# Head-pair values shifted and centred with tokens on partitions instead of by centring products

## The chip, the cores and the metric

The kernel runs on one core of one Trainium2 chip. The metric is the device time of one execution in microseconds (us); the time before is the median of three runs. Engine names follow the profile: PE is TensorE (PEld its weight loads), DVE is VectorE, ACT is ScalarE, POOL is GpSimd, SP is the engine whose queue issues nearly all DMAs.

## The reference, cut to what matters

One layer: a combined projection of a 256-token stream (4096 wide), sixteen heads of forgetting attention, thirty-two heads of an RWKV-7 recurrence of width 64, a SiLU gate, an output projection and a LayerNorm. The change touches the recurrence's values `vr`: the projected values are first mixed with those of the token before, and the recurrence's output is normalised over the 64 channels of each head.

```python
proj = einsum('bsd,dc->bsc', x, w_in)
rw_prev = pad(rw, one zero token in front)[:, :-1]
rw = rw + (rw_prev - rw) * mu_shift
S_t = S_{t-1} diag(decay_t) + (S_{t-1} a_t) b_t^T + v_t k_t^T ;  y_t = S_t r_t
mu = mean(y over the head's 64 channels)
y = (y - mu) * rsqrt(var + GN_EPS) * gn_gain + gn_bias
```

The output is linear in the values, so taking the mean over a head's 64 channels out of the values takes it out of `y` as well. The kernel does that: the recurrence runs on centred values, and no mean has to be taken of `y`. The bonus term uses the values uncentred.

## The kernel before, in words

The input projection is eight passes (n = 0 to 7) of four blocks (b = 0 to 3), each block 512 output columns. A block contracts 4096 in 16 steps of two 128-row tiles. Its weights come in 512 KB pieces, named `w<n>_<b>_<q>` and shown by the profile as `w_<q>`: SP fetches a piece into one of four raw buffers (`fetch`, L212), ACT rounds it to a high part (`split`, L139, four buffers, `w_<q>h`), DVE forms the rest (L140, three buffers, `w_<q>l`), and PE makes twelve products of a step out of them: x high by w high (L145), x low by w high (L146), x high by w low (L147), for two token halves and two tiles. With these buffers DVE can form the low part of a piece only when PE has left the piece three before it.

Block 0 of a pass gives r and k of two head groups, block 1 the recurrent values (columns 0 to 255) and the attention's values (256 to 511) with tokens on partitions, blocks 2 and 3 the rest. At a block's end ACT copies the sums to `bk` (L784 for block 1), and `unload` (L697) turns them to channels on partitions by PE transposes (`tr`, L711) and mixes in the token before (`lerp`, L256: ACT L257, DVE L258, tile `s`). This and everything else, the recurrence (`rwkv`, L464), its preparation (`prepare`) and the attention (`fox`), is written as generators that take a turn at each `slot` inside a block. A scheduler then sets the final order of each engine's instructions from that; each engine and the SP queue works strictly in its own order.

Where the change sits, in block 2 of each pass: `rwkv` makes 32 products `gp` (L476), then 32 products `vp` (L485) that turn the shifted values `s` back to tokens on partitions and centre them at once, their moving operand the constant `cent` (identity minus 1/64 inside a head). DVE masks `gp` into `gb` (L496) and `lt` (L504), ACT copies `vp` to `SV` and `UV` (L510, L511), DVE multiplies `bon` by `s` (L513), POOL scales `BK` (L479), PE transposes `BK` (`tp`, L521). SP carries `gb` to DRAM and back (`nd`, `Nb`, L499 and L500).

Of the kernel before, what the change touches and what calls it, by code (L numbers as in the profile page):

```python
# [10 lines left out]
F32 = mybir.dt.float32  # L11
# [3 lines left out]
ALU = mybir.AluOpType  # L15
AX = mybir.AxisListType

P = 128
S = 256
D = 4096  # L20
KT = D // P
G = 16
C = 64
NCH = S // C
HD = 64
# [25 lines left out]
C_ID = 0  # L51
C_MASK = 128
C_ONES = 256
C_CENT = 384
C_E = 512
C_SCAN = 640
C_ROW = C_SCAN + S
C_W = C_ROW + 2
# [3 lines left out]
def constants():  # L62
    p = np.arange(P)[:, None]
    s = p % C
    t = np.arange(C)[None, :]
    cst = np.zeros((P, C_W), np.float32)
    cst[:, C_ID : C_ID + P] = np.eye(P)
    cst[:, C_MASK : C_MASK + C] = s < t
    cst[:, C_MASK + C : C_MASK + 2 * C] = s <= t
    same = (np.arange(P)[:, None] // HD) == (np.arange(P)[None, :] // HD)  # L70
    cst[:, C_ONES : C_ONES + P] = same
    cst[:, C_CENT : C_CENT + P] = np.eye(P) - same / HD
    j = (p % NG) * NJ + np.arange(P)[None, :] // B
    cst[:, C_E : C_E + P] = j == np.arange(P)[None, :] % B
    cst[:, C_SCAN : C_SCAN + S] = (np.arange(S)[None, :] % C) != 0
    first = np.array([1, 1, 0, 1, 0], np.float32)
    cst[:5, C_ROW] = 2 * first - 1
    cst[:5, C_ROW + 1] = 1 - first
    return cst


@with_exitstack
def layer(ctx: ExitStack, tc: tile.TileContext, xt, xtok, w_lora, w_main, w_o, up, par, mulora, fbias, lng, lnb, cst, out):
    nc = tc.nc
    PS = bass.MemoryType.PSUM

# [6 lines left out]
    def pst(name):  # L93
        return ps.tile([P, 512], F32, tag="ps", name=name)

    cs = const.tile([P, C_W], F32, name="cs")
# [31 lines left out]

    ident = cs[:, C_ID : C_ID + P]
    ones = cs[:, C_ONES : C_ONES + P]  # L130
    cent = cs[:, C_CENT : C_CENT + P]

    def column(name, i):
        return prm[:, PAR.index(name), i : i + 1]
# [21 lines left out]
    for n, (k0, k1) in enumerate(pieces):  # L156
        for k in range(k0, k1):
            t = xpool.tile([P, 2, S], F32R, tag=f"x{k}", name=f"x{k}")
# [31 lines left out]
    def wait(n):  # L190
        for _ in range(n):
            yield
# [50 lines left out]
    rp = mid.enter_context(tc.tile_pool(name="rp", bufs=1))  # L243
# [116 lines left out]
    HALF = [slice(0, C), slice(C, P)]  # L360
# [5 lines left out]
        return t.rearrange("p a b -> p (a b)")  # L366

    rk = {}
    pairs = {}
    done = set()  # L370
    prepared = set()
# [92 lines left out]
    def rwkv(n):  # L464
# [7 lines left out]
        for u in range(2):  # L472
            for c in range(NCH):
                for j in range(2):
                    h = HALF[j]
                    nc.tensor.matmul(gp[u][j][:, c * P : (c + 1) * P], BK[h, u, c, :], lt[j][h, u, c, :], start=True, stop=True)  # L476
        v = vv[n]
        kept = BK[:, :, 0 : NCH - 1, :]
        nc.gpsimd.tensor_tensor(kept, kept, lc[:, :, 0 : NCH - 1].unsqueeze(3).to_broadcast([P, 2, NCH - 1, P]), ALU.mult)  # L479
        vp = pst(f"vp{n}")  # L480
        for u in range(2):
            for c in range(NCH):
                for j in range(2):
                    h, o = HALF[j], HALF[1 - j]
                    nc.tensor.matmul(vp[o, u * S + c * C : u * S + (c + 1) * C], v[:, u, c * C : (c + 1) * C], cent[:, h], start=True, stop=True)  # L485

        def m(rows):
            return cs[rows, C_MASK : C_MASK + P].unsqueeze(1).to_broadcast([C, NCH, P])

# [3 lines left out]
        for u in range(2):  # L493
            for j in range(2):
                h = HALF[j]
                nc.vector.tensor_tensor(gb[j][h, u], gv[u][j][h], m(h), ALU.mult)  # L496
            for a in range(4):
                o = B * (a % 2)
                nc.sync.dma_start(out=nd[u, a].rearrange("c r s -> r c s"), in_=gb[a // 2][B * a : B * (a + 1), u, :, o : o + B])  # L499
            nc.sync.dma_start(out=flat(nb[:, u]), in_=nd[u].rearrange("q c r s -> (q c) (r s)").unsqueeze(1).to_broadcast([16, NG, B * B]))  # L500
        for u in range(2):
            for j in range(2):
                o = HALF[1 - j]
                nc.vector.tensor_tensor(lt[j][o, u], gv[u][j][o], m(o), ALU.mult)  # L504
        SV = [rp.tile([P, 2, NCH, C], F32, tag=f"SV{j}", name=f"SV{j}_{n}") for j in range(2)]
        UV = [rp.tile([P, 2, NCH, C], F32, tag=f"UV{j}", name=f"UV{j}_{n}") for j in range(2)]
        for j in range(2):
            o = HALF[1 - j]
            vo = vp.rearrange("p (u c t) -> p u c t", u=2, t=C)[o]
            nc.scalar.copy(SV[j][o], vo)  # L510
            nc.scalar.copy(UV[j][o], vo)  # L511
            nc.gpsimd.memset(SV[j][HALF[j], :, 0, :], 0.0)
        nc.vector.tensor_tensor(flat(bon), flat(bon), flat(v), ALU.mult)  # L513
        for u in range(2):
# [9 lines left out]
        prod = rp.tile([P, 2, NJ, B], F32, tag="prod", name=f"prod{n}")  # L524
# [20 lines left out]
        for a in range(4):  # L545
            o = C * (a // 2) + B * (a % 2)
# [3 lines left out]
        for u in range(2):  # L550
            for c in range(NCH):
                for j in range(2):
                    a, b = slice(C * j, C * j + B), slice(C * j + B, C * j + C)
                    nc.tensor.matmul(qp[b, u * P + c * B : u * P + (c + 1) * B], gb[j][a, u, c, B:C], T[a, u, c, :], start=True, stop=True)
        Q = rp.tile([P, 2, NCH, B], F32, tag="xc", name=f"Q{n}")
        for j in range(2):
            b = slice(C * j + B, C * j + C)
# [27 lines left out]
        for c in range(NCH):  # L585
# [10 lines left out]
            if c < NCH - 1:  # L596
# [4 lines left out]
                for j in range(2):  # L601
                    h = HALF[j]
# [26 lines left out]
        vs = pst(f"vs{n}")  # L629
# [64 lines left out]

    unloading = []

    def unload(n, b, bk, vt):  # L697
        yield from wait(LAG)
        if b == 0:
            while n and 2 * n - 1 not in prepared:  # L700
                yield
        elif b == 2:
            while n and n - 1 not in done:
                yield
        fq = fk = None
        cols = BLOCKS[b]
        for h in range(len(cols) // 2):
            tr = pst(f"tr{n}_{b}_{h}")
            for t in range(2):
# [48 lines left out]
    res = None  # L758
# [16 lines left out]
    vt = None  # L775
    for n in range(G // 2):
        for b in range(4):
            acc = block(n, b)
            while unloading:
                slot()  # L780
            bk = rp.tile([P, 2, OB], F32, tag="bk", name=f"bk{n}_{b}")
            for m in range(2):
                if b == 1:
                    nc.scalar.copy(bk[:, m, : 2 * P], acc[m][:, : 2 * P])  # L784
                else:
                    nc.scalar.copy(bk[:, m, :], acc[m])
            if b == 1:
                while n and 2 * n - 1 not in foxed:
                    slot()
                vt = rp.tile([P, 2, 2 * P], F32, tag="vt", name=f"vt{n}")  # L790
                for m in range(2):
                    nc.scalar.copy(vt[:, m, :], acc[m][:, 2 * P :])
            unloading.append(n)
            side(unload(n, b, bk, vt))
# [104 lines left out]
def arrange(inputs):  # L899
    a = {n: np.asarray(v) for n, v in inputs.items()}  # L900
# [11 lines left out]
    tiles = np.stack([t.reshape(KT, P, G // 2, 2, P) for t in types])  # L912
    main = np.stack([np.stack([tiles[j, :, :, :, u] for j, u in c], 3) for c in cols])
    res["w_main"] = np.ascontiguousarray(main.transpose(3, 0, 2, 1, 4, 5)).reshape(G // 2, 4, P, KT, OB)
    wo = a["w_out"].reshape(2, G, P, NB, OB)
    res["w_o"] = np.ascontiguousarray(wo.transpose(3, 2, 1, 0, 4).reshape(NB, P, KT, OB))
    res["up"] = np.ascontiguousarray(np.stack([a["w_up"].reshape(LORA, G, P).transpose(1, 0, 2), a["a_up"].reshape(LORA, G, P).transpose(1, 0, 2)], 2))
# [26 lines left out]
```

## Time and profile before

| What | Value |
|---|---|
| Median of three runs | 1979.7 us (1979.61 to 1979.78) |
| Profiled execution | 1979.63 us |
| Its span in the trace | 1977.8 us, so 1.8 us lie around it |
| PE busy | 1966.3 us, 99% of the span |
| DVE, ACT, POOL busy | 1323.6, 1002.4, 34.3 us |
| DMA queue q1 | 64.3% of 16 engines' span |

Each number is of one profiled execution. A row of the timeline gives a start, a duration, the engine, the line of the kernel, what is written and read, and in brackets the engine's idle time just before it with what ended it. Products are pipelined on PE: a row's duration is longer than the distance to the next row's start, and the distance is what a product costs.

### The profile page before, as it was taken

The numbers are of one execution on the slowest core, as the hardware profiler recorded it, in microseconds if no ns is written. First come the engines' busy times: TensorE is split into PE (matmuls) and PEld (weight loads), VectorE is DVE, ScalarE is ACT, GpSimd is POOL, SyncE is SP. The second block draws the span as 40 slices with busy tenths as digits, with TensorE's granted clock in tenths as the row PEclk, the third lists the DMA queues.
The fourth block names the chain that finished last, engine by engine and source line by source line (L and its number), as shares of the span: only waits on it lengthen the run. The fifth ranks groups of instructions, "written<-read, shape, count | busy, mean of one in ns | idle before, by whom it ended". The sixth has DMA issues, their size and how long they took to land.

```text
span 1977.8 us, 28676 instructions
## 1 busy us (share of the span) xinstructions
PE 1966.3 (99%) x10624; PEld 1614.2 (82%) x10624; DVE 1323.6 (67%) x2091; ACT 1002.4 (51%) x1506; POOL 34.3 (2%) x82
## 2 busy tenths in 40 slices
PE   9999999999999999999999999999999999999998
PEld 7888788878887888788878887888788878888885
DVE  6678576857685768576857685768576856755555
ACT  6554564456445644564456445644564454433331
POOL 0100000000000000000000000000000000000000
PEclk9999999999999999999999999999999999999998
DMA  9566566656665666566656765676556777866664
GB/s 335 150 190 184 179 191 195 181 177 191 204 187 162 192 192 195 166 191 195 188 170 191 206 185 162 191 206 186 163 189 189 242 274 246 267 193 192 182 207 152
DMA packets 140429, 387.63 MB, mean 196 GB/s; under 512 B 32200, under 2 KB 42456, under 8 KB 140288
## 3 DMA queue, kind: packets, MB, share of 16 engines
q1 hardware_dynamic: 139856, 385.37, 64.3%
q8 instruction: 83, 1.36, 0.3%
q10 hardware_dynamic: 432, 0.43, 0.1%
q14 instruction: 58, 0.48, 0.1%
HBM read 371.82 MB, written 13.91 MB: 195 GB/s over the span
## 4 chain that ended last, share of the span: by engine, by line
PE 99%; DVE 1%; ACT 0%; DMA 0%; ACTq 0%; issue 0%; DVEq 0%; SPq 0%
PE acc L145 24%; PE acc L147 24%; PE acc L146 23%; PE oacc L754 6%; PE oacc L755 6%; PE oacc L756 6%; PE tr L711 1%; PE yp L616 1%; PE gp L476 1%; PE up L591 1%; PE rh L564 1%; PE sp L600 0%; PE vp L485 0%; DVE res L871 0%; PE accl L147 0%; PE tp L521 0%
## 5 line engine op out<-in xcount | busy, mean ns | idle before, releaser
L535 DVE TENSOR_REDUCE xc<-prod 128x8 f32<-128x16 f32 (+30 forms) x248 | 73.1, 295 | 6.1
L532 DVE TENSOR_TENSOR prod<-Nb,xc 128x8 f32<-128x8 f32 (+30 forms) x248 | 72.3, 292 | 7.1
L140 DVE TENSOR_TENSOR w_9l<-w,w_9h 128x1024 fp32r<-128x1024 f32 x31 | 38.1, 1228 | 46.1 <-ACT pT L670 29.0
L140 DVE TENSOR_TENSOR w_1l<-w,w_1h 128x1024 fp32r<-128x1024 f32 x31 | 37.9, 1224 | 35.4 <-PE acc L147 35.4
L140 DVE TENSOR_TENSOR w_0l<-w,w_0h 128x1024 fp32r<-128x1024 f32 x31 | 37.9, 1223 | 34.1 <-PE acc L147 25.4
L139 ACT CAST w_1h<-w 128x1024 fp32r<-128x1024 f32 x31 | 32.7, 1056 | 55.1 <-PE acc L146 38.7
L140 DVE TENSOR_TENSOR w_11l<-w,w_11h 128x1024 fp32r<-128x1024 f32 x31 | 38.0, 1225 | 33.6 <-PE acc L147 24.7
L140 DVE TENSOR_TENSOR w_3l<-w,w_3h 128x1024 fp32r<-128x1024 f32 x31 | 37.8, 1220 | 31.8 <-PE acc L147 31.8
L139 ACT CAST w_2h<-w 128x1024 fp32r<-128x1024 f32 x31 | 32.7, 1056 | 49.3 <-PE acc L146 45.5
L139 ACT CAST w_11h<-w 128x1024 fp32r<-128x1024 f32 x31 | 32.6, 1051 | 49.6 <-DMA w<-in_w_main_dram 22.9
L140 DVE TENSOR_TENSOR w_6l<-w,w_6h 128x1024 fp32r<-128x1024 f32 x31 | 37.8, 1221 | 28.5 <-ACT UV L594 13.9
L139 ACT CAST w_0h<-w 128x1024 fp32r<-128x1024 f32 x31 | 32.7, 1056 | 44.8 <-PE acc L146 38.7
L140 DVE TENSOR_TENSOR w_10l<-w,w_10h 128x1024 fp32r<-128x1024 f32 x31 | 37.9, 1224 | 26.0 <-PE acc L147 25.8
L139 ACT CAST w_13h<-w 128x1024 fp32r<-128x1024 f32 x31 | 32.7, 1054 | 43.0 <-PE acc L146 26.6
L140 DVE TENSOR_TENSOR w_2l<-w,w_2h 128x1024 fp32r<-128x1024 f32 x31 | 37.9, 1222 | 22.6 <-PE acc L147 22.4
L145 PE MATMUL acc<-w_4h,x 128*128 128x512 f32 x124 | 53.0, 428 | 0.0
L140 DVE TENSOR_TENSOR w_15l<-w,w_15h 128x1024 fp32r<-128x1024 f32 x31 | 37.8, 1220 | 22.3 <-PE acc L147 20.8
L140 DVE TENSOR_TENSOR w_12l<-w,w_12h 128x1024 fp32r<-128x1024 f32 x31 | 37.5, 1209 | 21.4 <-PE acc L147 21.4
L139 ACT CAST w_15h<-w 128x1024 fp32r<-128x1024 f32 x31 | 32.6, 1051 | 36.9 <-PE acc L146 35.3
L145 PE MATMUL acc<-w_1h,x 128*128 128x512 f32 x124 | 51.2, 413 | 0.0
L145 PE MATMUL acc<-w_6h,x 128*128 128x512 f32 x124 | 51.2, 413 | 0.0
L145 PE MATMUL acc<-w_2h,x 128*128 128x512 f32 x124 | 51.0, 411 | 0.0
(804 smaller groups left out, 6536.9 us busy)
## 6 DMA issues: line engine op xcount, KB each, us to landing
w<-in_w_main_dram SPq DMA_DIRECT2D x496, 512.0 KB
wo<-in_w_o_dram SPq DMA_DIRECT2D x128, 512.0 KB
Nb<-nd SPq DMA_DIRECT2D x16, 512.0 KB
wr<-in_w_main_dram SPq DMA_DIRECT2D x15, 512.0 KB
hd<-hl SPq DMA_DIRECT2D x29, 256.0 KB
h<-hd SPq DMA_DIRECT2D x29, 256.0 KB
res<-in_xtok_dram SPq DMA_DIRECT2D x16, 256.0 KB
xr<-in_xt_dram SPq DMA_DIRECT2D x15, 256.0 KB
```

The source lines that it names most:

```text
L139: nc.scalar.copy(hi[:, :n], src[:, :n])
L140: nc.vector.tensor_tensor(lo[:, :n], src[:, :n], hi[:, :n].bitcast(F32), ALU.subtract)
L145: nc.tensor.matmul(acc[:, :n], xs[k][:, 0, tt], hi[:, o : o + n], start=(k == 0), stop=False)
L146: nc.tensor.matmul(acc[:, :n], xs[k][:, 1, tt], hi[:, o : o + n], start=False, stop=False)
L147: nc.tensor.matmul(acc[:, :n], xs[k][:, 0, tt], lo[:, o : o + n], start=False, stop=(k == KT - 1))
L476: nc.tensor.matmul(gp[u][j][:, c * P : (c + 1) * P], BK[h, u, c, :], lt[j][h, u, c, :], start=True, stop=True)
L532: first = nc.vector.tensor_tensor(prod[:, :, :, s + 1 :], nb[:, :, s : s + 1, s + 1 :].to_broadcast([P, 2, NJ, w]), xc[:, :, :, s + 1 :], ...
L535: nc.vector.tensor_reduce(xc[:, :, :, s : s + 1], prod[:, :, :, s:], AX.X, ALU.add)
L564: nc.tensor.matmul(rh[HALF[j], u * C : (u + 1) * C], lt[j][:, u, c, 0:C], SV[j][:, u, c, :], start=True, stop=True)
L754: nc.tensor.matmul(acc, ht[k][:, 0, tt], hi[:, o], start=(k == 0), stop=False)
L755: nc.tensor.matmul(acc, ht[k][:, 1, tt], hi[:, o], start=False, stop=False)
L756: nc.tensor.matmul(acc, ht[k][:, 0, tt], lo[:, o], start=False, stop=(k == KT - 1))
```

## The change: what it does

The 32 products `vp` of each pass go, and with them the constant `cent` and the two ACT copies from `vp` to `SV`. In their place stands work on `bk` of block 1, with tokens on partitions:

- At the end of block 0, SP loads the mixing coefficients of the pass's 256 value columns into `muv` (128 KB, one DRAM row to all partitions). It takes the buffer that `prod` and `T` use later in the pass.
- At the end of block 1, POOL zeroes the first row of a new tile `vs`, and SP copies `bk` into `vs` one partition further: 127 partitions by 2 by 256 numbers (254 rows of 1 KB) in one transfer, and the one row that crosses from token 127 to token 128 in a second one.
- Two slots later POOL forms `vs = (vs - bk) * muv + bk` in three passes of 128x512.
- DVE sums `vs` over each head's 64 channels (`vm`, 128x8), and eight DVE instructions of 64x2x64 write `vs` minus a 64th of that into `SV`. ACT copies `SV` to `UV`.

The values with channels on partitions (`tr` and `lerp`) stay, since the bonus uses them.

```diff
-        vp = pst(f"vp{n}")
-        for u in range(2):
-            for c in range(NCH):
-                for j in range(2):
-                    h, o = HALF[j], HALF[1 - j]
-                    nc.tensor.matmul(vp[o, u * S + c * C : u * S + (c + 1) * C], v[:, u, c * C : (c + 1) * C], cent[:, h], start=True, stop=True)
...
+        vm = rp.tile([P, 2, 2, 2], F32, tag="vm", name=f"vm{n}")
+        vt = vs_[n].rearrange("p m (u j v) -> p m u j v", u=2, j=2)
+        nc.vector.tensor_reduce(vm.rearrange("p m u j -> p (m u j)"), vs_[n].rearrange("p m (a v) -> p (m a) v", v=HD), AX.X, ALU.add)
         for j in range(2):
             o = HALF[1 - j]
-            vo = vp.rearrange("p (u c t) -> p u c t", u=2, t=C)[o]
-            nc.scalar.copy(SV[j][o], vo)
-            nc.scalar.copy(UV[j][o], vo)
+            for c in range(2):
+                h = HALF[c]
+                for a in range(2):
+                    nc.vector.scalar_tensor_tensor(
+                        SV[j][o, :, 2 * a + c, :], vm[h, a, :, j].unsqueeze(2).to_broadcast([C, 2, HD]), -1.0 / HD, vt[h, a, :, j, :], ALU.mult, ALU.add
+                    )
+            nc.scalar.copy(UV[j][o], SV[j][o])
...
+    def token_values(n, bk):
+        p = bk[:, :, : 2 * P]
+        t = vs_[n]
+        nc.gpsimd.tensor_tensor(t, t, p, ALU.subtract)
+        nc.gpsimd.tensor_tensor(t, t, muvs[n].unsqueeze(1).to_broadcast([P, 2, 2 * P]), ALU.mult)
+        nc.gpsimd.tensor_tensor(t, t, p, ALU.add)
...
     def unload(n, b, bk, vt):
         yield from wait(LAG)
+        if b == 1:
+            token_values(n, bk)
...
+            if b == 0:
+                muvs[n] = rp.tile([P, 2 * P], F32, tag="prod", name=f"muv{n}")
+                nc.sync.dma_start(out=muvs[n], in_=muv[n : n + 1, :].to_broadcast([P, 2 * P]))
             if b == 1:
+                vs_[n] = rp.tile([P, 2, 2 * P], F32, tag="vs", name=f"vs{n}")
+                nc.gpsimd.memset(vs_[n][0:1, 0, :], 0.0)
+                nc.sync.dma_start(out=vs_[n][1:P], in_=bk[0 : P - 1, :, : 2 * P])
+                nc.sync.dma_start(out=vs_[n][0:1, 1, :], in_=bk[P - 1 : P, 0, : 2 * P])
```

The order on three engines, in pass n = 1. On PE, at the gp products of block 2, before:

```order
L476 MATMUL gp_1_1_3233<-lt_1_2786,BK_2784 128x128
L485 MATMUL vp_3251<-cs,s_2_3171 64x64 x16
L145 MATMUL acc_2_0_3134<-w_2_4h,x_364 128x512
L146 MATMUL acc_2_0_3134<-w_2_4h,x_364 128x512
L147 MATMUL acc_2_0_3134<-w_2_4l,x_364 128x512
```

The same place on PE with the change:

```order
L474 MATMUL gp_1_0_3241<-lt_1_2787,BK_2786 128x128
L474 MATMUL gp_1_1_3242<-lt_1_2788,BK_2786 128x128
L142 MATMUL acc_2_0_3140<-w_2_4h,x_364 128x512
L143 MATMUL acc_2_0_3140<-w_2_4h,x_364 128x512
L144 MATMUL acc_2_0_3140<-w_2_4l,x_364 128x512
```

The products `vp` are gone (a row counts pairs); nothing else on PE has moved, here or elsewhere. Next DVE, at the start of block 2, before (`w_2_4l` is the low part of block 2's piece 4, `s_2` the values with channels on partitions):

```order
L140 TENSOR_TENSOR w_2_3l<-w_2_3_3154,w_2_3h 128x1024
L258 SCALAR_TENSOR_TENSOR s_2_3171<-tr_1_0_3166,prm,s_2_3171 128x255
L140 TENSOR_TENSOR w_2_4l<-w_2_4_3182,w_2_4h 128x1024
L258 SCALAR_TENSOR_TENSOR s_2_3171<-tr_1_0_3166,prm,s_2_3171 128x255
L513 TENSOR_TENSOR bon_2787<-bon_2787,s_2_3171 128x512
L140 TENSOR_TENSOR w_2_5l<-w_2_5_3200,w_2_5h 128x1024
L140 TENSOR_TENSOR w_2_6l<-w_2_6_3218,w_2_6h 128x1024
L496 TENSOR_TENSOR gb_838<-gp_0_0_3230,cs 64x512
```

The same place on DVE with the change:

```order
L137 TENSOR_TENSOR w_2_3l<-w_2_3_3160,w_2_3h 128x1024
L255 SCALAR_TENSOR_TENSOR s_2_3180<-tr_1_0_3175,prm,s_2_3180 128x255
L500 TENSOR_REDUCE vm_3284<-vs_3133 128x8
L255 SCALAR_TENSOR_TENSOR s_2_3180<-tr_1_0_3175,prm,s_2_3180 128x255
L137 TENSOR_TENSOR w_2_4l<-w_2_4_3191,w_2_4h 128x1024
L506 SCALAR_TENSOR_TENSOR SV_1_3280<-vm_3284,vs_3133 64x2x64 x4
L506 SCALAR_TENSOR_TENSOR SV_1_3281<-vm_3284,vs_3133 64x2x64
L137 TENSOR_TENSOR w_2_5l<-w_2_5_3209,w_2_5h 128x1024
L506 SCALAR_TENSOR_TENSOR SV_1_3281<-vm_3284,vs_3133 64x2x64 x3
L511 TENSOR_TENSOR bon_2789<-bon_2789,s_2_3180 128x512
L137 TENSOR_TENSOR w_2_6l<-w_2_6_3227,w_2_6h 128x1024
L487 TENSOR_TENSOR gb_838<-gp_0_0_3239,cs 64x512
```

The sum over `vs` now stands ahead of the low parts of pieces 4, 5 and 6, and the eight `SV` writes between them. Last the SP queue at the end of block 1, before:

```order
L216 DMA w_2_3_3154<-in_w_main_dram 128x1024
L216 DMA w_2_4_3182<-in_w_main_dram 128x1024
L216 DMA w_2_5_3200<-in_w_main_dram 128x1024
L216 DMA w_2_6_3218<-in_w_main_dram 128x1024
L216 DMA w_2_7_3307<-in_w_main_dram 128x1024
```

The same place on the SP queue with the change:

```order
L213 DMA w_2_4_3191<-in_w_main_dram 128x1024
L213 DMA w_2_5_3209<-in_w_main_dram 128x1024
L803 DMA vs_3133<-bk_1_3130 1x16x16
L802 DMA vs_3133<-bk_1_3130 127x2x256
L213 DMA w_2_6_3227<-in_w_main_dram 128x1024
L213 DMA w_2_7_3307<-in_w_main_dram 128x1024
```

The two transfers into `vs` stand between the fetches of pieces 5 and 6 of block 2. The row of one partition is written as sixteen parts of sixteen numbers; the 127 partitions stand as they are.

More of the change, by code (lines that the diff above doesn't have):

```diff
@@ L53 @@
 C_ONES = 256
-C_CENT = 384
-C_E = 512
+C_E = 384
 C_SCAN = 640
@@ L71, in constants @@
     cst[:, C_ONES : C_ONES + P] = same
-    cst[:, C_CENT : C_CENT + P] = np.eye(P) - same / HD
     j = (p % NG) * NJ + np.arange(P)[None, :] // B
@@ L82, in layer @@
 @with_exitstack
-def layer(ctx: ExitStack, tc: tile.TileContext, xt, xtok, w_lora, w_main, w_o, up, par, mulora, fbias, lng, lnb, cst, out):
+def layer(ctx: ExitStack, tc: tile.TileContext, xt, xtok, w_lora, w_main, muv, w_o, up, par, mulora, fbias, lng, lnb, cst, out):
     nc = tc.nc
@@ L130, in layer @@
     ones = cs[:, C_ONES : C_ONES + P]
-    cent = cs[:, C_CENT : C_CENT + P]
     def column(name, i):
@@ L368, in layer @@
     rk = {}
+    vs_ = {}
     pairs = {}
@@ L695, in layer @@
     unloading = []
+    muvs = {}
+    def token_values(n, bk):
[4 more added lines that the diff above has]
+        nc.gpsimd.tensor_tensor(t, t, p, ALU.add)
     def unload(n, b, bk, vt):
         yield from wait(LAG)
+        if b == 1:
+            token_values(n, bk)
         if b == 0:
@@ L914, in arrange @@
     res["w_main"] = np.ascontiguousarray(main.transpose(3, 0, 2, 1, 4, 5)).reshape(G // 2, 4, P, KT, OB)
+    res["muv"] = np.ascontiguousarray(a["mu_shift"][4096:6144].reshape(G // 2, 2 * P))
     wo = a["w_out"].reshape(2, G, P, NB, OB)
```

## The prediction

> **What bounds the kernel now.** I read the page first: the busy times and the chain that ended last.
>
> ```profile
> PE 1966.3 (99%) x10624; PEld 1614.2 (82%) x10624; DVE 1323.6 (67%) x2091; ACT 1002.4 (51%) x1506; POOL 34.3 (2%) x82
> PE 99%; DVE 1%; ACT 0%; DMA 0%; ACTq 0%; issue 0%; DVEq 0%; SPq 0%
> ```
>
> PE bounds it: it never runs dry between the first weights and the tail, and every other engine works under its cover. So a product taken off PE is worth its pitch on PE, and any other work costs nothing as long as PE's next weights are ready. Two questions follow: what the vp products cost on PE, and how much cover DVE, ACT, POOL and SP have where the new work goes. I read both in pass 1, start of block 2, which repeats in every pass; the timeline of PE there:
>
> ```profile
> 317.53 0.39 PE L147 MATMUL acc<-w_15l,x 128*128 128x512 f32 x1
> 329.35 0.39 PE L146 MATMUL acc<-w_4h,x 128*128 128x512 f32 x1
> 329.58 0.39 PE L147 MATMUL acc<-w_4l,x 128*128 128x512 f32 x1
> 330.57 2.06 PE L476 MATMUL gp<-lt,BK 64*128 64x128 f32 x32
> 332.56 1.15 PE L485 MATMUL vp<-cs,s 128*64 128x64 f32 x32
> 333.64 0.50 PE L145 MATMUL acc<-w_4h,x 128*128 128x512 f32 x1
> 337.88 0.39 PE L145 MATMUL acc<-w_6h,x 128*128 128x512 f32 x1
> 341.51 0.39 PE L145 MATMUL acc<-w_7h,x 128*128 128x512 f32 x1
> ```
>
> Block 1's last product starts at 317.53; at 329.58 PE first needs the low part of piece 4, and at 341.51 it begins piece 7. The 32 vp products cost 333.64 - 332.56 = 1.08 us. The timelines of DVE and of ACT in the same stretch:
>
> ```profile
> 318.01 1.23 DVE L140 TENSOR_TENSOR w_2l<-w,w_2h 128x1024 fp32r<-128x1024 f32 x1 [1.49 <-PE acc L147]
> 322.98 0.48 DVE L258 SCALAR_TENSOR_TENSOR s<-tr,prm,s 128x255 f32<-128x255 f32 x1 [1.02 <-ACT s L257]
> 323.86 1.23 DVE L140 TENSOR_TENSOR w_4l<-w,w_4h 128x1024 fp32r<-128x1024 f32 x1 [0.40 <-PE acc L147]
> 325.52 0.69 DVE L513 TENSOR_TENSOR bon<-bon,s 128x512 f32<-128x512 f32 x1
> 331.77 1.41 DVE L496 TENSOR_TENSOR gb<-gp,cs 64x512 f32<-64x512 f32 x2 [1.16 <-PE gp L476]
> 337.29 1.21 DVE L140 TENSOR_TENSOR w_7l<-w,w_7h 128x1024 fp32r<-128x1024 f32 x1
> ```
>
> ```profile
> 318.68 0.37 ACT L784 COPY bk<-acc 128x256 f32<-128x256 f32 x1
> ...
> 333.76 0.58 ACT L510 COPY SV<-vp 64x512 f32<-64x512 f32 x1 [3.56 <-PE vp L485]
> ```
>
> The low part of piece 4 is done at 325.09, and PE needs it at 329.58: 4.5 us of cover. That of piece 7 is done at 338.50, needed at 341.51 + 0.46 = 341.97: 3.5 us.
>
> **What goes.** Eight times 1.08 us of PE, 8.6 us on the path. ACT loses two copies of 0.58 us per pass and its 3.56 us wait for vp; it is not on the path, so nothing.
>
> **What comes, work alone.** POOL's nearest row, and DVE's (the sums and a write into SV):
>
> ```profile
> L479 POOL TENSOR_TENSOR BK<-BK,lc 128x768 f32<-128x768 f32 x8 | 11.8, 1472 | 303.8 <-DVE gb L496 303.8
> L661 DVE TENSOR_REDUCE fst<-lg 128x1 f32<-128x256 f32 x16 | 6.5, 409 | 0.0
> L661 DVE TENSOR_REDUCE fst<-lg 128x1 f32<-128x128 f32 x16 | 4.4, 276 | 0.0
> L607 DVE TENSOR_TENSOR SV<-sp,sl 64x128 f32<-64x128 f32 x32 | 9.2, 287 | 8.3 <-PE sp L600 8.1
> ```
>
> A POOL pass over 128x512 is 1.472 x 512/768 = 0.98 us, three are 2.9 (at most 4.4, the unscaled row). The sum over 512 numbers is 0.409 + 2 x 0.133 = 0.68 us; eight SV writes at 0.287 are 2.3 us. With `vs` there in time, all of it fits in DVE's idle time: no cost. Of SP's three new transfers `muv` has a whole block until its use; its 128 packets, at the dearest price below (179 ns), keep the 16 engines for 1.4 us, with several pieces under way: nothing. The two into `vs` wait on SP for ACT's copy, with the fetch of piece 6 queued behind; but that one had to wait for the low part of piece 2 in any case, done at 318.01 + 1.23 = 319.24. The two issues before it, 0.8 us, are hidden by the time until PE uses piece 6 at 337.88.
>
> **The transfer into vs, the deciding term.** It can't start before ACT's second copy of `bk` is done at 318.68 + 0.37 = 319.05. DVE's sum waits for POOL, POOL for this transfer; and behind the sum, in DVE's strict order, stands the low part of piece 4, which PE needs at 329.58. So the 4.5 us of cover are no longer cover for short work but the budget of a chain: two issues, a landing, POOL, the sum.
>
> How long does it take to land 254 rows of 1 KB? First the rows of the DMA view, in three short windows (299.5 to 300: pieces alone; 304 to 304.5: nearly only the 1 KB rows of `upt`; 203 to 204: mostly one DRAM row sent to all partitions), then an issue on SP and SP's wait for a transfer to land:
>
> ```profile
> DMA packets 50, 0.20 MB, mean 410 GB/s; under 512 B 0, under 2 KB 0, under 8 KB 50
> q1 hardware_dynamic: 50, 0.20, 99.4%
> ...
> DMA packets 25, 0.02 MB, mean 45 GB/s; under 512 B 6, under 2 KB 24, under 8 KB 25
> q1 hardware_dynamic: 25, 0.02, 13.0%
> ...
> DMA packets 106, 0.17 MB, mean 166 GB/s; under 512 B 13, under 2 KB 79, under 8 KB 106
> q1 hardware_dynamic: 106, 0.17, 118.8%
> ...
> 300.35 0.42 SPq L378 DMA_DIRECT2D upt<-in_up_dram  x1
> SPq L543 <- DMA td<-xc: 15.0, 8, 3.2
> ```
>
> A packet occupies one engine of the 16 for share x 16 x window / packets: 0.994 x 8000/50 = 159 ns for 4 KB, so 40 ns per KB; 0.13 x 8000/25 = 42 ns for the 1 KB rows; 1.188 x 16000/106 = 179 ns where one DRAM row is read over and over. Ours reads SBUF row by row, so I take 42 ns. Over 16 engines that is 254/16 x 42 ns = 0.7 us; on one engine 254 x 42 ns = 10.6 us. No transfer of before has a row count like 127, so the trace doesn't show which. I take one engine: 127 is prime and can't be cut into equal parts, and the order hands it over whole, while it cuts the one-row transfer beside it into sixteen parts. Every large transfer of before has 128, 96 or 32 rows.
>
> The Trainium skill speaks against this change at just this place: "DMA: Bandwidth & Descriptors", section "Why a DMA increments its semaphore by 16 and not by 1", says that such a DMA runs on the largest number of engines up to 16 that divides its slowest dimension, with 127 partitions on one as an example. At the page's roughly 27 GiB/s an engine I estimate 9.0 us instead of 10.6, and the sum below would be about 2035. No run here shows it yet.
>
> So vs lands at 319.05 + 2 x 0.42 (issues) + 1.9 (15.0/8, the mean wait for a landing) + 10.6 = 332.4. POOL is done at 335.4 (ACT's copies to `prod`, which now wait for `muv` to be free, and the second `s` and the high parts of pieces 5 and 6 behind them, are released a POOL pass earlier and ready in time), DVE's sum at 336.1, the second `s` at 336.6 (0.48), the low part of piece 4 at 337.8 (1.23). PE, stopped since 329.58, has lost 8.2 us.
>
> Then PE goes from 337.8 to piece 7 in 0.99 (to gp), 1.99 (gp) and 341.51 - 333.64 = 7.87: it is there at 348.65 and needs the low part at 349.1. DVE gets there at 337.8 + 2.3 (SV) + 0.69 (bon) + 2.46 (pieces 5 and 6) + 5.52 (masks, 331.77 to 337.29) + 1.21 = 350.0, a second stop of 0.9, with which piece 7 would begin at 349.5, 8.0 us later than before. POOL's next work, BK's scaling for `tp`, waits for gp (340.8) and for the SV writes (341.3) and is done by 342.8; `tp` stands behind piece 5 and half of piece 6 on PE: no cost.
>
> PE's clock covers that second stop and adds a little. The windows of the tail, the third number from the end of a row (PEclk) being the clock, and the warm-up:
>
> ```profile
> core 0: us, PE busy (x) PEld busy (x) DVE busy (x) ACT busy (x) POOL busy (x), PEclk, DMA share, GB/s
> 1962.00:1964.00 2.00, 1.60 (x6) 0.69 (x5) 1.79 (x4) 0.00 (x0) 0.00 (x0) 1.00 0.40 162
> 1964.00:1966.00 2.00, 0.28 (x1) 0.09 (x1) 1.47 (x7) 0.29 (x1) 0.00 (x0) 0.64 0.25 100
> 1966.00:1968.00 2.00, 1.66 (x5) 1.26 (x5) 2.00 (x4) 0.26 (x1) 0.00 (x0) 0.50 0.14 55
> 1.31 2.74 PE L106 MATMUL warmup<-idle 128*128 128x512 bf16 x6 [1.31 <-POOL idle L103]
> ```
>
> With about 2 us of idle time the clock falls to 0.50, and at the start six products of 512 columns took 2.74 us, 0.457 each, against the 0.23 from 329.35 to 329.58. So an 8 us stop is followed by at least 2.7 us at half speed, a loss of 1.4 us. Then PE begins piece 7 at 350.05, needs the low part at 350.5 and finds it ready at 350.0. Shift of a pass: 350.05 - 341.51 = 8.5 us, vp's saving included. Nothing later in the pass wins it back, as PE is the bound; DVE, ACT and SP shift along. Pass 0 has the same order with two BK writes more behind the sum, within half a microsecond of this.
>
> **Sum.** 1979.6 (the profiled execution, 1979.63; the median is 1979.7) + 8 x 8.5 = 1979.6 + 68 = 2048. Bounds of this case: 40 ns a packet and no landing time, no clock loss but the second stop, gives 8.0 - 1.9 - 0.4 = 5.7 a pass, 2025; a landing of 3.2 us (the longest) and twice the clock loss gives 8.5 + 1.3 + 1.4 = 11.2, 2069. At 179 ns a packet it would be 35 us more a pass, about 2330; I keep that as a far end only.
>
> **Rivals.**
>
> Spread transfer, faster: the 254 rows go over 16 engines. Then vs lands at 319.05 + 0.84 + 1.9 + 0.7 = 322.5, POOL is done at 325.5, piece 4's low part at 327.9, before 329.58; piece 7's at 327.9 + 12.2 = 340.1, needed at 340.9 with vp gone. PE never stops, and the whole saving shows: 1979.6 - 8.6 = 1971. It decides by a landing before about 323.3, 4.2 us after the copy. For it: a 256 KB transfer of 128 rows would do this. Against it: 127. Chance 0.13.
>
> Two engines: 254 rows as two lots of 127. The transfer takes 5.3 us, PE stops about 3 us at piece 4 and 0.9 at piece 7, and I take no loss of clock: 8.0 - 5.3 = 2.7 a pass, 2001. Nothing in the order cuts the transfer so. Chance 0.05.
>
> The stop isn't PE's: the transfer takes 10.6 us, but DVE's order is of no matter, as PE would stop only for piece 6, fetched behind `vs` on the same queue. Piece 6 would land 8 x 159 ns behind vs, at 333.7, its two parts be ready 2 x 1.23 later at 336.2 and be needed at 337.88 - 1.08 = 336.8: no stop, 1971 again. It fails if the sum really stands ahead of piece 4, as the order has it. Chance 0.02, counted with the first.
>
> **How the numbers follow.** One engine 0.80 (2025 to 2069 by its own bounds, and some tens more if packets are slower), spread or hidden 0.15, two engines 0.05. To leave out no more than 2 in 10, the range takes in the two-engine case below and a margin above for slow packets: 1996 to 2095. A measurement of this kernel can tell about 0.2% (4 us) from no change. Faster by more takes the spread case with hardly a stop, 0.12; a spread case that gives its 8.6 us back in small stops, 0.03 within 0.2%; slower 0.85.
>
> **What would show it.** Right: one wait of about 8 us on PE before a product of w_4l in every pass, the row of DVE's sum (the line of `vm`) waiting for POOL, POOL's first pass waiting for `vs` about 13 us after ACT's copy, PEclk below 1 behind each stop, and the mean DMA share near 1/16 for 10 us in which only `vs` moves. Wrong: POOL starting within 4 us of the copy, and PE at 99% as before.

## The result and the profile after

| | before | after |
|---|---|---|
| median, 4 runs each (us) | 1979.65 (1978.91 to 1979.78) | 2082.16 (2079.56 to 2083.15) |
| ratio, 95% interval | | 1.0516 (1.0502 to 1.0529) |
| profiled execution: time, span (us) | 1979.63, 1977.8 | 2079.56, 2077.7 |
| mean granted PE clock | 0.997 | 0.974 |

The change costs 102.5 us, 5.2%. The forecast was 2048, its range 1996 to 2095. The page of the changed kernel, the busy times and the chain that ended last by engine and by line:

```profile
PE 1976.6 (95%) x10368; PEld 1618.9 (78%) x10368; DVE 1341.4 (65%) x2163; ACT 994.6 (48%) x1490; POOL 67.6 (3%) x114
PE 89%; DMA 6%; POOL 1%; DVE 1%; issue 1%; ACT 0%; DVEq 0%; POOLq 0%; SPq 0%
```

PE makes 256 products fewer and is busy longer, because part of its work ran at half clock. It is no longer the whole chain: a DMA holds 6% of it, about 125 us, where before its share was 0%. The waits view says for whom:

```profile
POOL vs L700 <- DMA vs<-bk: 319.1, 8, 54.0
DVE vm L500 <- POOL vs L702: 120.4, 8, 15.2
ACT prod L526 <- POOL vs L701: 114.6, 8, 15.1
PE acc L144 <- DVE w_4l L137: 88.8, 8, 11.5
```

Rows 1, 2 and 4 are the chain of the forecast, eight times each: POOL waits for the transfer into `vs`, DVE's sum (`vm`) for POOL, and PE for the low part of piece 4, which stands behind the sum on DVE. The first row's long total is harmless (POOL has nothing else to do); the last row is the cost. Row 3 is a second branch: ACT's copy to `prod` waits for POOL too, and ACT's second part of `s` stands behind it. Pass 1 in the timelines of ACT, POOL, DVE and PE, one stretch of each (start, duration, then what ran, in brackets the idle time before it and what ended that):

```profile
331.52 0.37 ACT L793 COPY bk<-acc 128x256 f32<-128x256 f32 x1
...
347.31 1.26 POOL L700 TENSOR_TENSOR vs<-vs,bk 128x512 f32<-128x512 f32 x1 [39.50 <-DMA vs<-bk]
...
349.99 1.26 POOL L702 TENSOR_TENSOR vs<-vs,bk 128x512 f32<-128x512 f32 x1
...
351.29 0.69 DVE L500 TENSOR_REDUCE vm<-vs 128x8 f32<-128x512 f32 x1 [14.98 <-POOL vs L702]
351.89 0.47 DVE L255 SCALAR_TENSOR_TENSOR s<-tr,prm,s 128x255 f32<-128x255 f32 x1
352.28 1.22 DVE L137 TENSOR_TENSOR w_4l<-w,w_4h 128x1024 fp32r<-128x1024 f32 x1
...
353.55 0.80 PE L144 MATMUL acc<-w_4l,x 128*128 128x512 f32 x1 [10.97 <-DVE w_4l L137]
```

ACT's copy is done at 331.89; the values land 15.4 us later; POOL and DVE need 6.2 us more; PE stands still for 10.97 us. What moved the values is read in the DMA view, here 335 to 340:

```profile
DMA packets 103, 0.12 MB, mean 24 GB/s; under 512 B 0, under 2 KB 102, under 8 KB 102
q1 hardware_dynamic: 102, 0.10, 6.5%
```

A share of 6.5% of 16 engines is one engine (1/16 is 6.25%), with 102 packets of 1 KB in 5 us, one each 49 ns. So the transfer of 127 rows does run on one engine, and the rule of the Trainium skill that the prediction named ("DMA: Bandwidth & Descriptors", section "Why a DMA increments its semaphore by 16 and not by 1") agrees with the trace. The page's rate (section "Specifications"), roughly 27 GiB/s an engine, gives an estimate of 9.0 us for 254 rows; the 49 ns measured here give 12.4. Last the windows view, whose third number from the end is the granted clock:

```profile
353.50:356.00 2.50, 2.45 (x8) 1.61 (x10) 2.43 (x7) 0.61 (x1) 0.00 (x0) 0.50 0.51 129
357.00:358.00 1.00, 1.00 (x22) 1.00 (x20) 1.00 (x2) 0.89 (x3) 0.10 (x1) 1.00 0.78 135
```

Behind the stop PE runs at half clock, and is at full clock again some 3.5 us after it started.

Where all of it went is best seen by the step of PE from the first product of one weight piece to the first of the next. Against before, one step of each pass grew, piece 4 of block 2, in passes 0 to 7 by 13.29, 11.67, 12.73, 11.65, 12.65, 13.22, 11.98 and 12.83 us. That is 100.0 together, against 99.9 between the two profiled executions: nothing is left to find elsewhere.

### The profile page after: what moved, and what is told of

The parts are those of the page before. It is cut to its first block, busy times and chain, and to the rows that moved or that the text cites. A ratio compares the mean times of both kernels' runs of the same rounds, so it can differ in the third digit from the quotient of the medians.

```text
span 2077.7 us, 28297 instructions
## 1 busy us (share of the span) xinstructions
PE 1976.6 (95%) x10368; PEld 1618.9 (78%) x10368; DVE 1341.4 (65%) x2163; ACT 994.6 (48%) x1490; POOL 67.6 (3%) x114
## 4 chain that ended last, share of the span: by engine, by line
PE 89%; DMA 6%; POOL 1%; DVE 1%; issue 1%; ACT 0%; DVEq 0%; POOLq 0%; SPq 0%
PE acc L142 22%; PE acc L144 21%; PE acc L143 21%; DMA vs<-bk 6%; PE oacc L763 6%; PE oacc L765 6%; PE oacc L764 6%; PE gp L474 1%; PE tr L720 1%; PE yp L614 1%; PE up L589 1%; PE rh L562 1%; POOL vs L702 0%; POOL vs L700 0%; POOL vs L701 0%
## 5 line engine op out<-in xcount | busy, mean ns | idle before, releaser
L144 PE MATMUL acc<-w_4l,x 128*128 128x512 f32 x124 | 53.8, 434 | 88.8 <-DVE w_4l L137 88.8
L144 PEld LDWEIGHTS acc<-w_4l,x 128*128 128x128 f32 x124 | 25.3, 204 | 97.6 <-DVE w_4l L137 92.1
L500 DVE TENSOR_REDUCE vm<-vs 128x8 f32<-128x512 f32 x8 | 5.5, 686 | 120.4 <-POOL vs L702 120.4
```

The lines of the kernel that those rows point to most:

```text
L144: nc.tensor.matmul(acc[:, :n], xs[k][:, 0, tt], lo[:, o : o + n], start=False, stop=(k == KT - 1))
```

## The experiments

Theory: the transfer is slow because it runs on one engine, and it costs because DVE's sum, behind it, is queued ahead of the low part of piece 4. Rivals: the time goes into holding back the weight fetches behind the transfer in SP's queue, whatever DVE does; or into POOL's and DVE's added work itself. The kernel before ran beside each group, at 1979.5 to 1979.7; all ratios are to it.

**1. The transfer cut in two, 112 and 15 rows.** The large part can now be spread.

```diff
-                nc.sync.dma_start(out=vs_[n][1:P], in_=bk[0 : P - 1, :, : 2 * P])
+                nc.sync.dma_start(out=vs_[n][1:113], in_=bk[0:112, :, : 2 * P])
+                nc.sync.dma_start(out=vs_[n][113:P], in_=bk[112 : P - 1, :, : 2 * P])
```

> The 127-row transfer cut into 112 and 15 rows, the rest of the change kept. Theory (the one-engine transfer holds DVE's sum and so PE): 112 rows go over 16 engines, 15 over 15, vs lands within 4 us of ACT's copy instead of 15.4, PE doesn't stop at piece 4, and the whole saving of the vp products shows: 1971, ratio to before 0.996. Rival (POOL's three passes of 1.26 us and the new DVE work hold PE by themselves): PE still stops in block 2, and the time is 1985 or more.

Measured: 1973.9 us, ratio 0.9971 (0.9959 to 0.9982). The timelines of ACT, POOL and DVE in pass 1:

```profile
320.11 0.36 ACT L793 COPY bk<-acc 128x256 f32<-128x256 f32 x1
...
323.75 1.30 POOL L700 TENSOR_TENSOR vs<-vs,bk 128x512 f32<-128x512 f32 x1 [27.36 <-DMA vs<-bk]
325.13 1.29 POOL L701 TENSOR_TENSOR vs<-vs,muv 128x512 f32<-128x512 f32 x1
326.50 2.15 POOL L702 TENSOR_TENSOR vs<-vs,bk 128x512 f32<-128x512 f32 x1
...
325.29 2.21 DVE L137 TENSOR_TENSOR w_4l<-w,w_4h 128x1024 fp32r<-128x1024 f32 x1 [0.40 <-PE acc L144]
```

The values land 3.3 us after the copy, 12 us sooner, and 108 us of 2082 are gone. Two things changed, though: the scheduler now also put the sum, which ran at 328.68, behind the low part of piece 4. Run 5 changes the order without the cut, run 8 uses one order with both cuts; no run has the cut with the order of the changed kernel.

**2. The cut at 96 and 31 rows.** The same edit with 97 for 113 and 96 for 112; the smaller part, 31 rows, again on one engine.

> The same transfer cut into 96 and 31 rows; 31 is prime like 127. Theory (a row count without a divisor goes to one engine): 62 packets of 47 ns on one engine, 2.9 us, on top of the 3.4 us that a landing takes besides its packets; POOL starts 6 to 7 us after the copy, some 3 us later than with 112 and 15. The chain then ends at about piece 4's or 7's need: 1971 to 1980. Rival (the row count is of no matter, only the number of rows): POOL starts as early as with 112 and 15.

Measured: 1999.2 us, ratio 1.0099 (1.0084 to 1.0114). The values landed 7.5 us after the copy (expected 6 to 7) against 3.3 in run 1, so the row count matters; the time was far off. The longest of PE's waits, and the timelines of ACT and DVE in pass 1:

```profile
PE acc L144 <- DVE w_7l L137: 14.7, 8, 2.1
```

```profile
332.51 0.30 ACT L526 COPY prod<-cs 128x128 f32<-128x128 f32 x1 [6.31 <-POOL vs L701]
332.72 0.47 ACT L254 ACTIVATE s<-tr,omm 128x256 f32<-128x256 f32 x1
...
333.22 0.48 DVE L255 SCALAR_TENSOR_TENSOR s<-tr,prm,s 128x255 f32<-128x255 f32 x1 [4.88 <-ACT s L254]
333.88 0.69 DVE L500 TENSOR_REDUCE vm<-vs 128x8 f32<-128x512 f32 x1 [0.18 <-POOL vs L702]
...
345.03 1.21 DVE L137 TENSOR_TENSOR w_7l<-w,w_7h 128x1024 fp32r<-128x1024 f32 x1
```

A second queue is at work, which the expectation had left out: ACT's copy to `prod` waits for POOL (`muv` lies in the same buffer), ACT's part of `s` stands behind it, DVE's part of `s` waits for that, and pieces 5, 6 and 7 are queued behind. Read alone, this doesn't say whether the orders or the transfer made the stops; run 8 does.

**3. The products alone taken out.** The kernel before without `vp`; its output is not the reference's, since the values it copies to `SV` and `UV` are neither turned nor centred.

```diff
-                    nc.tensor.matmul(vp[o, u * S + c * C : u * S + (c + 1) * C], v[:, u, c * C : (c + 1) * C], cent[:, h], start=True, stop=True)
...
-            vo = vp.rearrange("p (u c t) -> p u c t", u=2, t=C)[o]
+            vo = v.rearrange("p u (c t) -> p u c t", t=C)[o]
```

> The kernel before without the vp products: ACT copies the shifted values with channels on partitions into SV and UV, so the values are neither turned nor centred; nothing else is changed. The term of the sum alone: 8 x 1.08 = 8.6 us less on PE, 1971.0. Rival (a product taken off PE is filled by waiting for weights): 1979.7, no change.

Measured: 1970.6 us, ratio 0.9955 (0.9938 to 0.9971). The products are worth 9.0 us. This kernel is the floor for the rest: what a variant of the change takes above 1970.6 is the price of getting the values by another way.

**4. The transfer alone.** The kernel before, plus the two transfers into `vs`, with no reader.

```diff
+                vsn = rp.tile([P, 2, 2 * P], F32, tag="vs", name=f"vs{n}")
+                nc.gpsimd.memset(vsn[0:1, 0, :], 0.0)
+                nc.sync.dma_start(out=vsn[1:P], in_=bk[0 : P - 1, :, : 2 * P])
+                nc.sync.dma_start(out=vsn[0:1, 1, :], in_=bk[P - 1 : P, 0, : 2 * P])
```

> The kernel before with the two transfers into vs at the end of block 1 and nothing that reads vs. In the profile of the changed kernel the fetch of piece 6, issued right behind, began to move only about 8 us later, when half of the packets of vs were gone, and landed behind them. If that hold costs by itself: piece 6 lands 16 us after the copy, its low part keeps DVE from the masks, piece 7's low part is about 2.5 us late, 8 x 2.5 = 20 us: 2000. Rival (the transfer costs only through the sum that waits for it): 1979.7.

Measured: 2012.6 us, ratio 1.0169 (1.0154 to 1.0184). A transfer that nobody waits for costs 33 us. PE's longest wait, then the timelines of ACT and DVE in pass 1: the copy of `bk`, the conversion of piece 6 and its low part:

```profile
PE tp L521 <- DVE lt L504: 18.8, 16, 1.5
```

```profile
322.71 0.37 ACT L784 COPY bk<-acc 128x256 f32<-128x256 f32 x1
...
340.44 1.05 ACT L139 CAST w_6h<-w 128x1024 fp32r<-128x1024 f32 x1 [9.65 <-DMA w<-in_w_main_dram]
...
341.52 1.23 DVE L140 TENSOR_TENSOR w_6l<-w,w_6h 128x1024 fp32r<-128x1024 f32 x1 [9.61 <-ACT w_6h L139]
```

Piece 6, queued on SP behind the transfer, lands 17.4 us after the copy. DVE's masks `gb` and `lt` are queued behind its low part, and PE waits for them before `tp`; the expectation had the masks right but put the stop at piece 7 and the time at 2000. So the rival of the held fetch is real; in the changed kernel it doesn't show, because PE already stands at piece 4 while piece 6 is late.

**5. The order alone.** The changed kernel with its one-engine transfer; the sum, the `SV` writes and the `UV` copies moved behind the wait for the decay products, kept there, and ACT's copies to `prod` and `xc` kept in place.

```diff
-        nc.vector.tensor_reduce(vm.rearrange("p m u j -> p (m u j)"), vs_[n].rearrange("p m (a v) -> p (m a) v", v=HD), AX.X, ALU.add)
...
         yield from wait(W["d1"])
+        tc.keep_in_program_order(nc.vector.tensor_reduce(vm.rearrange("p m u j -> p (m u j)"), vs_[n].rearrange("p m (a v) -> p (m a) v", v=HD), AX.X, ALU.add))
...
-            nc.scalar.copy(prod[:, u], ev)
+            tc.keep_in_program_order(nc.scalar.copy(prod[:, u], ev))
```

> The changed kernel with its transfer as it is (127 rows, all on one DMA engine), but VectorE's sum over the shifted values, its eight centring instructions and ScalarE's two UV copies come only after the slope of the chain is through (the wait that stands ahead of the decay products), and ScalarE's two copies of the decay prefix keep their place, so that neither engine queues work for the weight pieces behind GpSimd's three passes. If the order on VectorE made the stop at piece 4 (11.5 us a pass by the waits view of the changed kernel): that stop goes, and what is left is the late fetch of piece 6, 3 to 4.4 us a pass as in the run of the transfer alone, perhaps with a late BK scaling on GpSimd: 2000, between 1992 and 2010. If the stop is due to the late values themselves, whoever waits for them: it stays, about 2080.

Measured: 2015.7 us, ratio 1.0185 (1.0171 to 1.0199). The stop at piece 4 is gone, and 66 us with it: DVE's and ACT's orders made it, together. No run moved the sum alone. In the changed kernel ACT's second part of `s`, behind the copy to `prod`, ran only at 350.35, and DVE's part of `s` needs it and stands ahead of the low part of piece 4; with the sum out of the way that would have been done at an estimated 350.35 + 0.47 + 0.47 + 1.22 = 352.5 instead of 353.5. PE's waits now:

```profile
PE tp L508 <- POOL BK L477: 10.9, 8, 1.4
PE acc L144 <- DVE w_6l L137: 7.8, 8, 1.0
PE acc L142 <- ACT w_6h L136: 4.5, 7, 0.8
```

What is left, 45 us above the floor, sits mostly in PE's step of piece 6 (32 of 47 us between the profiled executions), which also holds `tp`: PE waits there for POOL's scaling of `BK` and for piece 6, whose fetch is late as in run 4. The expected 2000 was too low by a false sum: the 33 us of run 4 were taken against a kernel that still had the `vp` products. A late fetch sets a time of arrival, and PE's work ahead of it hides in the wait; against the floor run 4 cost 42 us, which leaves 3 of the 45 open.

**6. The same, with the transfer from ACT's queue** (`nc.scalar.dma_start` in place of `nc.sync.dma_start`).

> The late order, and the 127-row transfer issued from ScalarE's queue and not from SyncE's, which carries the fetches of the weights. If the fetch of piece 6 was late because it stood behind the transfer in SyncE's own queue: it comes in time, and the time is 1971 to 1980. If one busy DMA engine holds up every fetch that has a share on it, whichever queue that share came from: piece 6 is late as before, and the time is that of the late order with SyncE's queue, about 2000, at least within 6 us of it.

Measured: 2050.6 us, ratio 1.0360 (1.0346 to 1.0374). Neither number, so the trace has to answer. PE's longest wait, then the timelines of ACT, POOL and PE in pass 1 (the copy of `bk` is done at 327.00):

```profile
PE tp L508 <- POOL BK L477: 61.5, 8, 8.1
```

```profile
334.61 1.03 ACT L136 CAST w_6h<-w 128x1024 fp32r<-128x1024 f32 x1
...
348.53 1.26 POOL L701 TENSOR_TENSOR vs<-vs,bk 128x512 f32<-128x512 f32 x1 [45.61 <-DMA vs<-bk]
352.43 1.47 POOL L477 TENSOR_TENSOR BK<-BK,lc 128x768 f32<-128x768 f32 x1
...
353.95 1.97 PE L508 MATMUL tp<-cs,BK 128*128 128x128 f32 x8 [7.70 <-POOL BK L477]
```

The question asked is answered: piece 6 is there within 7.6 us of the copy and nobody waits for it, so its lateness came from standing in SP's own queue. SP's issue of its fetch takes 0.34 us here, and took 7.73 us in run 5. The DMA view of 328 to 334 shows the difference. Run 5, one queue, one busy engine:

```profile
q1 hardware_dynamic: 121, 0.12, 6.5%
```

This run, SP's queue (q1) and ACT's (q10) side by side:

```profile
q1 hardware_dynamic: 282, 1.03, 59.3%
q10 hardware_dynamic: 55, 0.06, 2.9%
```

The fetches flow, but the transfer moves about half as many packets, 55 instead of 121, and lands after 21.5 us instead of 16.4. That uncovered a third queue: POOL's scaling of `BK` stands behind its three passes over `vs`, and PE's transposes `tp` behind that. The Trainium skill ("DMA: Bandwidth & Descriptors", section "Issuing engines are not separate DMA queues") says that issuing from several engines saves only the time of the issues, which is usually small. Here that time was large, 7.4 us of one issue, and piece 6 came 7.6 us behind the copy instead of 17.3 (run 5).

**7. ACT's queue, with POOL's order mended too.** As run 6, with `BK`'s scaling kept ahead of the three passes.

```diff
-        nc.gpsimd.tensor_tensor(kept, kept, lc[:, :, 0 : NCH - 1].unsqueeze(3).to_broadcast([P, 2, NCH - 1, P]), ALU.mult)
+        tc.keep_in_program_order(nc.gpsimd.tensor_tensor(kept, kept, lc[:, :, 0 : NCH - 1].unsqueeze(3).to_broadcast([P, 2, NCH - 1, P]), ALU.mult))
+        token_values(n, vb[n])
```

> The late order on VectorE and ScalarE and the 127-row transfer from ScalarE's queue, as in the run of 2050.6 us; now GpSimd's BK scaling also keeps its place ahead of its three passes over the values. The transfer stays on one DMA engine and lands some 20 us after the copy. If the cost of a slow transfer lies only in what is queued behind it or behind its readers, nothing is left of the 70 us: 1971 to 1976, with no PE wait before the transposes of BK. If the slow transfer costs by itself, or the fetches suffer from the shared engine: 1990 or more, with waits for a DMA at pieces 6 to 11.

Measured: 2003.5 us (2001.1 to 2008.5), ratio 1.0123 (1.0108 to 1.0138). POOL's order was worth 47 us here, and PE's wait before `tp` is gone, but the floor is not reached. SP's timeline in pass 1, the DMA view of 342 to 344, SP's wait for the transfer and PE's longest wait:

```profile
336.28 10.26 SPq L491 DMA_DIRECT2D nd<-gb  x8
...
348.29 2.50 SPq L213 DMA_DIRECT2D w<-in_w_main_dram  x4
```

```profile
DMA packets 42, 0.04 MB, mean 21 GB/s; under 512 B 1, under 2 KB 42, under 8 KB 42
q10 hardware_dynamic: 42, 0.04, 6.0%
...
SPq L491 <- DMA vs<-bk: 51.8, 8, 6.7
PE acc L142 <- ACT w_11h L136: 8.2, 8, 2.0
```

The eight small writes `nd` take 10.3 us to issue. Three of them are issued by 337.8; the fourth waits for the transfer to land and is issued at 344.35, and `Nb` and the fetch of piece 11 stand behind it, so that PE stops at pieces 10 and 11. Write and transfer have no tile in common. But in the trace's records SP waits, in each of the eight passes, for the semaphore that tells of the transfer's landing, and the fourth write then uses the same one. So the stops at pieces 10 and 11 are traced to a semaphore that the program uses again while the slow transfer still holds it; no run took that reuse away. The expectation's second case has the number, but neither of its reasons. Run 6 has the same wait (52.8 us in all), under PE's stop at `tp`. In run 8 the same two rows read:

```profile
331.14 3.77 SPq L490 DMA_DIRECT2D nd<-gb  x8
...
337.17 1.49 SPq L213 DMA_DIRECT2D w<-in_w_main_dram  x2
```

**8. The cut transfers with the late order.** The edits of runs 1 and 2, each with that of run 5.

> The late order, with the transfer cut in two of 112 and 15 rows, so that it is spread over many DMA engines. With values that land 3 us after the copy, the order should hardly matter: 1971 to 1974. If the 3.1 us that the cut alone left in pass 0 came from the sum's early place on VectorE: 1971, with pass 0 as in the kernel without value products; if they come from the transfer or from GpSimd's passes: 1974 as with the cut alone.

> The late order, with the transfer cut in two of 96 and 31 rows. The cut alone gave 1999.2 with stops at piece 7, where VectorE's second token-shift difference waited for a sigmoid behind ScalarE's copy of the decay prefix, which waited for GpSimd. If that chain of orders made the stops: they go, 1971 to 1976. If the transfer itself makes them, by holding back the fetches: 1995 to 2000, with a wait for a DMA at piece 6 or 7.

Measured: with 112 and 15 rows (the rows just shown) 1971.7 us, ratio 0.9961 (0.9948 to 0.9973); with 96 and 31 rows 1971.3 us, ratio 0.9961 (0.9946 to 0.9976). Both are at the floor; of PE's steps with 112 and 15 rows none differs from run 3 by over 0.15 us, so the 3.1 us of run 1, nearly all of it in pass 0, are gone too. So the 28 us between run 2 and its late twin came from what the orders on ACT and DVE queue behind the values, and not from fetches that the transfer holds back. Either one is 0.4% faster than the kernel before, and faster than the changed one; the two can't be told apart.

**9. SP's queue, with all three orders late.** The edit of run 7 on the kernel of run 5.

> The same orders on all three engines, with the transfer in SyncE's queue as in the changed kernel. What is left is then the queue alone, as in the run that only added the transfer (33 us): 2004, between 1998 and 2012, with PE's wait at piece 6 and ScalarE's wait for its fetch. If the 12 us by which the late order with SyncE's queue (2015.7) lay above that came from the BK scaling behind the values, they go; if they stay, 2016.

Measured: 2018.0 us, ratio 1.0189 (1.0172 to 1.0206): as run 5, so POOL's order is worth nothing with this queue, and the 2004 was the false sum of run 5 again. PE's waits moved from `tp` to piece 7:

```profile
PE acc L144 <- DVE w_7l L137: 16.9, 8, 2.1
```

**10. Half the transfer, alone.** Run 4 with one plane only, 127 packets instead of 254.

```diff
-                nc.sync.dma_start(out=vsn[1:P], in_=bk[0 : P - 1, :, : 2 * P])
+                nc.sync.dma_start(out=vsn[1:P, 0], in_=bk[0 : P - 1, 0, : 2 * P])
```

> The kernel before plus half the transfer, one plane of 127 rows of 1 KB, read by nobody. In the changed kernel the other 15 DMA engines stood until some 117 of the 254 packets were left. If the queue runs ahead by about that many packets of one engine, the fetch behind 127 packets starts on the other engines after some 10 packets, within 2 us of the first: piece 6 is in time and the time is within 4 us of the kernel before. If the other engines wait for a share of the transfer (half of it), they start after some 64 packets, 3 to 5 us later; if for all of it, 6 us later.

Measured: 1979.54 us in one run, beside 1979.70. It costs nothing that one run could tell, and no step of PE differs from before by over 0.16 us. ACT's timeline in pass 1:

```profile
318.58 0.37 ACT L784 COPY bk<-acc 128x256 f32<-128x256 f32 x1
...
327.80 1.05 ACT L139 CAST w_6h<-w 128x1024 fp32r<-128x1024 f32 x1 [1.15 <-DMA w<-in_w_main_dram]
```

Piece 6 comes 8.9 us after the copy, not 17.4, and PE doesn't need it yet. (One plane needs only the first of ACT's two copies, so the transfer was issued 2 us sooner too, at 316.89.)

## Why the prediction was right, and where its sizes were off

**The products** (8 x 1.08 = 8.6 us): run 3 gives 9.0.

**One engine** (chance 0.80): right, by the share of 6.5%; and run 1, whose values land 12 us sooner, shows that it was the row count.

**The mechanism**, a stop before a product with the low part of piece 4 in every pass and nowhere else: right, by the waits and the steps; run 5, which moves DVE's and ACT's orders, takes the stop away. The share of ACT's order, which by the estimate at run 5 would have kept nearly all of the stop, the prediction had only as "ready in time".

**The size**, 8.5 us a pass forecast, 11.67 in pass 1 and 12.5 on the mean. Three terms were too small:

| term, pass 1 (us) | forecast | measured | from |
|---|---|---|---|
| copy done to POOL's start | 13.3 | 15.4 | 331.89 to 347.31 |
| POOL's three passes | 2.9 | 3.9 | 347.31 to 351.25 |
| sum, `s`, low part of piece 4 | 2.4 | 2.3 | 351.25 to 353.50 |
| stop | 8.2 | 10.97 | PE's row |
| lost behind the stop | 1.4 | 1.8 | 17.69 - 10.97 - 4.94 |

The last row is the step of piece 4 (17.69) less the stop and less the same step in run 3 (4.94). The transfer's packets were priced at 42 ns each: they came 49 ns apart in the window above, and 52 on the mean of all 254, from 333.35 to 346.63. POOL's pass was scaled by the elements from the scaling of `BK`, whose second operand holds one number for 128 columns: each of the three took 1.26 us and not 0.98, though the one by `muv` too has an operand that repeats (for both token halves), so what makes the difference stays open. Both errors add straight to the stop, since the budget of 10.5 us between ACT's copy and PE's need was right (10.7, from 331.89 to 342.58). The second stop, 0.9 us at piece 7, was to be covered by the slow clock behind the first, and it was: the low part of piece 7 was done at 365.16, and PE needed it at 366.47. The 2082 lies above 2069, the bound that the prediction had worked out from rows for one engine; only the margin for slow packets, up to 2095, took it in.

**Rival, spread transfer** (1971): its price was right, 1973.9 with the order as the scheduler then made it and 1971.7 with the late one; its condition wasn't met.

**Rival, the stop isn't PE's** (piece 6, 1971): the step that failed is "8 x 159 ns behind `vs`, no stop", and with it "the two issues before it, 0.8 us, are hidden" in the price of the work alone. Behind a one-engine transfer piece 6 lands 17.4 us after the copy and costs 33 us with no other change (run 4). That the forecast didn't suffer was luck: PE stood at piece 4 while piece 6 was late. With the late orders the time is 2016 (run 5), not 1971.

**POOL**: the claim that `BK`'s scaling behind the three passes costs nothing held in the changed kernel, where PE stops earlier anyway. It is no general truth: in run 6 that order was worth 47 us.

## What to carry to other kernels

A transfer of a row count that can't be cut evenly, here 127, can run on a single DMA engine; cut in 112 and 15 rows, with one more issue and the order that the scheduler then made, it was 108 us faster. What a late result costs is decided by what the schedulers queue behind its readers on each engine, so follow the order on every engine that touches it, and on the queue that carries it, before calling a wait hidden; here it was DVE, ACT, POOL and SP in turn, and last a semaphore that the slow transfer held. And a stop set by an arrival can't be added to work that PE does ahead of it: that work is inside the stop.

## What the hardware showed unexpectedly

**A queue held by one engine.** The fetch of piece 6 was issued at 332.76 in the changed kernel, but until 341 only one engine was busy. The DMA view of 332.4 to 341:

```profile
DMA packets 179, 0.18 MB, mean 21 GB/s; under 512 B 27, under 2 KB 174, under 8 KB 178
q1 hardware_dynamic: 178, 0.17, 6.6%
```

From 341 to 345:

```profile
q1 hardware_dynamic: 343, 1.06, 87.5%
```

When the other engines started, 174 - 27 = 147 of the transfer's 254 packets were through and 107 left. SP's timeline shows where the fetch stood: its issue itself took 7.72 us, and that of the fetch before it 0.33.

```profile
332.76 7.72 SPq L213 DMA_DIRECT2D w<-in_w_main_dram  x1
```

By its end, at 340.48, the same count gives 135 packets, and 119 left. In run 5 the issue took 7.73 us, and 119 were left at its end. In run 10 the DMA behind the 127 packets is the transfer of the one row, and its issue (0.59 us in the changed kernel) was held too:

```profile
317.65 2.56 SPq L791 DMA_DIRECT2D vs<-bk  x1
```

At its end 9 packets were gone and 118 left, much as the expectation of that run had it. In every pass of the changed kernel and of runs 4, 5, 9 and 10 the issue behind the transfer ended with 113 to 122 packets of the transfer left. So in these kernels SP's queue ran ahead of the one engine by some 120 packets and no further. No run varied the size of the packets or the number of engines, and the reason stays open.

**A subtraction on DVE and a pass on POOL shut each other out.** In run 1 the low part of piece 4, 1.23 us alone, took 2.21 us when it started at 325.29 inside a POOL pass that ended at 326.42, and POOL's next pass, 1.26 us in the changed kernel, took 2.15 as DVE was busy until 327.50. Each is longer by about what the other still had to run. Not every DVE instruction does this: DVE's part of `s`, inside the POOL pass of 323.75, took its usual 0.48 us, and that pass 1.30.
